# Expert weights in rows of 8 KB, and a nineteenth slot in layer 2's ring of weights

## The chip, the cores and the metric

One core of one Trainium2 chip runs the whole program. The metric is the device time of one execution in microseconds; less is better. The times given are the median of three timed runs, and one further execution was recorded by the hardware profiler.

## What is computed

Two layers of a diffusion backbone over 512 latent tokens of 1024 channels, with 256 context tokens beside them in the first layer. Each layer has four token mixers that are merged by gates, and then a mixture of 16 experts, in which each expert chooses its tokens (64 of the latent tokens, 32 of the context). What the change touches are the weights of the experts:

```
def expert_choice_moe(h, w_router, w_g, w_u, w_d):
    ...
    aff = jax.nn.softmax((h @ w_router).astype(jnp.float32), axis=-1)
    gate, idx = lax.top_k(jnp.swapaxes(aff, 1, 2), cap)
    ...
    xe = h[bidx, idx]
    hid = jax.nn.silu(jnp.einsum('becd,edf->becf', xe, w_g)) * jnp.einsum('becd,edf->becf', xe, w_u)
    ye = jnp.einsum('becf,efd->becd', hid, w_d) * gate[..., None].astype(h.dtype)
    return jnp.zeros_like(h).at[bidx, idx].add(ye)
```

Each of the three matrices of an expert is 1024 by 1024 in float32, 4 MB. One layer's experts are 16 x 3 x 4 MB = 192 MB, all of which has to come from HBM once per layer.

## The kernel before

The experts go in eight pairs, p = 0 to 7. Each pair has a gate, an up and a down product. A weight tile is 1 MB: 256 rows of one expert's matrix, held as 128 partitions of 2 rows of 4 KB. So a product of a pair takes 8 tiles (four quarters of two experts), a pair 24, and a layer 192. `gemm` runs over the quarters; a quarter takes the two experts' tiles, and when it is done it asks for two more tiles (`load_ew(st_ew.i + 2)`, L1117).

`ExpertStream` (L975 on) sets which tile goes where. Its list `loads` has the tiles in the order gate 0, up 0, and then for each pair: gate of the next, down of this one, up of the next. Its list `ring` names the buffers that the tiles use in turn. In layer 1 (`has_c`, the context tokens are there) these are three "raw" buffers and ten of the blocks "b0" to "b9". In layer 2 they are 18: three "raw", "b4", "Xc", then nine blocks, "b10" and three of the tag "ew" in a pool that lives from the output projection to the end of the experts. The tile of number i takes the buffer i modulo 18, and its DMA can go once the matmuls have read the tile that was there.

All of these loads are issued by SyncE (SP), in one order, and those behind one that waits wait too. `ew.load(ew.early)` (L737) asks for the first of them while the output projection is still being computed ("early" is the length of the ring's first part: 5 in layer 2). The coroutine `moe` asks for more when the layer's router runs (L1015), four more that are tied to the router's last result by a one-element copy (L1016), and the rest of the ring tied to the first one-hot matrix of the selection (L1255).

In layer 2 TensorE works on a pair as: up product of p, with the adding of the previous pair's result between its matmuls; gate product of p + 1; down product of p. The down product's result is scaled on VectorE (L1144), split into two parts on ScalarE and VectorE (L201, L202) and added to the tokens by matmuls with one-hot matrices (L1159, L1160). The tokens of a pair come by an indirect DMA from GpSimd (L1070, "xg"). The last down product (p = 7) takes its tiles by halves of columns (`last_gemm`, L1132): such a tile holds 256 rows of 512 columns of both experts, and is loaded by two DMAs of 512 KB.

The inputs may be laid out on the host: `_layout` makes the arrays that lie in HBM. Before, the three expert arrays are passed as they are, [2, 16, 1024, 1024]. The weights of the mixers ("w_in_t", "w_gate_t") are stored there tile by tile already, with 8 KB for each partition.

GpSimd's own DMAs (indirect gathers, stores of the normalized tokens at L800, copies of key parts at L367 and L368) have their descriptors in a scratch area at the start of each partition of SBUF, 16,384 bytes of each by default.

Of the kernel before, what the change touches and what calls it, by code (L numbers as in the profile page):

```python
# [19 lines left out]
L = 2  # L20
D = 1024
KC = 8
NE = 16
# [17 lines left out]
def backbone(ctx: ExitStack, tc: tile.TileContext, A: dict, out: bass.AP):  # L41
    nc = tc.nc
# [4 lines left out]
    def nm(p):  # L47
        cnt[0] += 1
        return f"{p}_{cnt[0]}"

    def pool(name, space=None):
        kw = {"space": space} if space is not None else {"reuse_waits": "tile"}
        return tc.tile_pool(name=nm(name), bufs=1, **kw)

    P0 = ctx.enter_context(pool("p0"))
# [3 lines left out]
    def T_(p, shape, dt=F32, tag=None, bufs=1):  # L59
        t = tag or "t"  # L60
        return p.tile(shape, dt, name=nm(t), tag=tag or nm("u"), bufs=bufs)
# [65 lines left out]
    class Parts:  # L127
        def __init__(self, tiles, per):
            self.tiles, self.per = tiles, per
# [845 lines left out]
    class ExpertStream:  # L975
        def __init__(self, l, has_c):
            self.l, self.pool, self.i, self.t, self.has_c, self.stack = l, None, 0, {}, has_c, ExitStack()
            self.ring = [("raw", 3)] * 3 + ([] if has_c else [("b4", 1), ("Xc", 1)])
            self.early = len(self.ring)
            self.ring += [(f"b{i}", 1) for i in (0, 1, 2, 3, 5, 6, 7, 8, 9)]  # L980
            self.ring += [("b4", 1)] if has_c else [("b10", 1)] + [("ew", 3)] * 3
            self.size = len(self.ring)
            order = [(0, 0), (0, 1)]
            for p in range(8):
                order += ([(p + 1, 0)] if p < 7 else []) + [(p, 2)] + ([(p + 1, 1)] if p < 7 else [])
            self.loads = [(p, mt, qt, e) for p, mt in order for qt in range(4) for e in range(2)]
# [6 lines left out]
        def load(self, upto, after=None):  # L993
            while self.i < min(upto, len(self.loads)):
                key = p, mt, qt, e = self.loads[self.i]
                tag, bufs = self.ring[self.i % self.size]
                t = T_(self.pool if tag == "ew" else P0, [128, 2, 1024], tag=tag, bufs=bufs)
                if after is not None:
                    V.tensor_copy(t[:, 0, 0:1], after)
                src = A[("w_exp_gate", "w_exp_up", "w_exp_down")[mt]]  # L1000
                if (p, mt) == (7, 2):
                    t = t.rearrange("p k (b m) -> p k b m", b=2)
                    rows, cols = (2 * qt + e) % 4 * 256, (2 * qt + e) // 4 * 512
                    parts = [(t[:, ex], src[self.l, 2 * p + ex, rows:rows + 256, cols:cols + 512]) for ex in range(2)]
                else:
                    parts = [(t, src[self.l, 2 * p + e, qt * 256:(qt + 1) * 256, :])]
                for dst, rw in parts:
                    nc.sync.dma_start(dst, rw.rearrange("(k p) m -> p k m", p=128))
                self.t[key] = t
                self.i += 1  # L1010

# [303 lines left out]
    for l in range(L):  # L1315
        n2d = [DR.tile([st.n, D], F32, name=nm("n2"), tag=nm("n2")) for st in (LAT, CTX)]
        ew = ExpertStream(l, l < L - 1)
# [11 lines left out]
def _layout(inp):  # L1329
    f = {k: np.asarray(v) for k, v in inp.items()}  # L1330
    c_ = np.ascontiguousarray
    a = {}
    a["x"] = c_(f["x"][0])
    a["ctx"] = c_(f["ctx"][0])
    cond = np.stack([f["c"][0], f["c_ctx"]])
    a["w_ada"] = c_(f["w_ada"])
    a["b_ada"] = c_(f["b_ada"])

    def pairs(w):
        n = w.shape[2] // 256  # L1340
        return c_(w.reshape(L, KC, 128, n, 2, 128).transpose(0, 3, 2, 4, 1, 5).reshape(L, n, 128, 2048))

    a["w_in_t"] = pairs(f["w_in"])
    a["w_gate_t"] = pairs(f["w_gate"])
    a["w_proj"] = c_(np.concatenate([f["w_pa"], f["w_pb"], f["w_pc"], f["w_pd"]], axis=1))
    a["w_o"] = c_(f["w_o"])
    a["w_sp_t"] = c_(f["w_sp"].transpose(0, 3, 1, 2))
    a["b_sp"] = c_(f["b_sp"])
    a["sgu_ln_g"] = c_(f["sgu_ln_g"])
    a["sgu_ln_b"] = c_(f["sgu_ln_b"])  # L1350
    a["lam_v"] = c_(np.stack([f["lam_q1"], f["lam_k1"], f["lam_q2"], f["lam_k2"]], axis=1))
    for k in ("ln1_g", "ln1_b", "ln2_g", "ln2_b", "w_exp_gate", "w_exp_up", "w_exp_down"):
        a[k] = c_(f[k])
    a["w_router_c"] = c_(f["w_router"].reshape(L, KC, 128, NE).transpose(0, 2, 1, 3))
    cs = np.zeros((128, C_N), np.float32)
    cs[:, C_ID:C_ID + 128] = np.eye(128)
    cs[:, C_TRI:C_TRI + 128] = np.triu(np.ones((128, 128)), 1)
    cs[:, C_IOTA:C_IOTA + 64] = np.arange(64)
    cs[:, C_TOK] = np.arange(128)
    cs[:, C_COND:C_BG] = cond.reshape(2, KC, 128).transpose(2, 1, 0).reshape(128, 16)  # L1360
    cs[:, C_BG:C_CONV] = f["b_gate"].reshape(L * 32, 128).T
    cs[:, C_CONV:C_SUB] = f["conv_w"].reshape(L, 3, 2, 128).transpose(3, 0, 2, 1).reshape(128, 6 * L)
    cs[:, C_SUB:C_LB] = f["subln_g"].T
    cs[:, C_LB:C_N] = f["ln1_b"].reshape(L * KC, 128).T
    for b in range(2):
        cs[:, C_HALF + b] = (np.arange(128) // 32) % 2 == b
    a["consts"] = cs
    t = np.arange(512)
    inv = (np.float32(10000.0) ** (-np.arange(0, 32, 2, dtype=np.float32) / np.float32(32))).astype(np.float32)
    row, col = (t // 64).astype(np.float32), (t % 64).astype(np.float32)  # L1370
    ang = np.concatenate([row[:, None] * inv, col[:, None] * inv], axis=-1).astype(np.float32)
    cos, sin = np.cos(ang).astype(np.float32), np.sin(ang).astype(np.float32)
    p = np.arange(128)
    fr = (p % 64) // 2
    sgn = np.where(p % 2 == 0, -1.0, 1.0).astype(np.float32)
    a["rope"] = c_(np.stack([cos[:, fr].T, sin[:, fr].T * sgn[:, None]], axis=1))
    k = np.arange(64)
    th = 2 * np.pi * ((k[:, None] * k[None, :]) % 64) / 64
    bd = np.zeros((128, 2, 128))
    for g in range(2):  # L1380
        s = slice(64 * g, 64 * g + 64)
        bd[s, 0, s] = np.cos(th)
        bd[s, 1, s] = -np.sin(th)
    a["dft_d"] = c_(bd.reshape(128, 256).astype(np.float32))
    for nme, n in (("l", 512), ("c", 256)):
        k = np.arange(n)
        th = 2 * np.pi * ((k[:, None] * k[None, :]) % n) / n
        cm = np.stack([np.cos(th), np.sin(th)]) / math.sqrt(n * 64)
        a["dft_" + nme] = c_(cm.reshape(2, n // 128, 128, n).transpose(0, 2, 1, 3).reshape(2, 128, -1).astype(np.float32))
    return a  # L1390
# [16 lines left out]
```

## Time and profile before

| | |
|---|---|
| median of three runs | 2636.95 us (2631.57, 2636.95, 2638.67) |
| profiled execution, its own time | 2632.32 us |
| profiled execution, span | 2630.5 us |
| TensorE busy | 2461.1 us, 94% |
| VectorE, ScalarE busy | 1084.4 us, 725.7 us |
| granted TensorE clock, mean | 0.978 |
| DMA | 628.20 MB in 155,842 packets, mean 239 GB/s |

A busy TensorE counts matmuls in flight, so it need not be at its peak. The shares are averages over stages with different limits: layer 1's expert stage lies at about 890 to 1515 us, layer 2's mixers behind it, and layer 2's expert stage from about 2135 us to the end.

### The profile page before, as it was taken

The numbers are of one execution on the slowest core, as the hardware profiler recorded it, in microseconds if no ns is written. First come the engines' busy times: TensorE is split into PE (matmuls) and PEld (weight loads), VectorE is DVE, ScalarE is ACT, GpSimd is POOL, SyncE is SP. The second block draws the span as 40 slices with busy tenths as digits, with TensorE's granted clock in tenths as the row PEclk, the third lists the DMA queues.
The fourth block names the chain that finished last, engine by engine and source line by source line (L and its number), as shares of the span: only waits on it lengthen the run. The fifth ranks groups of instructions, "written<-read, shape, count | busy, mean of one in ns | idle before, by whom it ended". The sixth has DMA issues, their size and how long they took to land. (4 is left out here: it accounts for less than half of the span.)

```text
span 2630.5 us, 35463 instructions
## 1 busy us (share of the span) xinstructions
PE 2461.1 (94%) x14575; PEld 1479.2 (56%) x14575; DVE 1084.4 (41%) x2310; ACT 725.7 (28%) x1400; POOL 210.4 (8%) x247
## 2 busy tenths in 40 slices
PE   6899999999999999999999889999999969988886
PEld 4788876788787333333333277678878733332322
DVE  4656787343237412222221468734322732111114
ACT  3644656332233201010000265633223310000001
POOL 0102121001011000000000002100101100000000
PEclk8899999999999899999999999999999979999998
DMA  7586535222325798888898443552232589999996
GB/s 280 188 296 250 196 111 174 77 96 83 110 80 201 299 408 323 320 307 339 339 349 320 170 136 106 179 202 97 83 110 80 199 349 409 409 409 409 409 409 242
DMA packets 155842, 628.20 MB, mean 239 GB/s; under 512 B 11680, under 2 KB 14112, under 8 KB 137760
## 3 DMA queue, kind: packets, MB, share of 16 engines
q1 hardware_dynamic: 141872, 588.78, 59.3%
q0 software_dynamic: 7520, 23.07, 2.9%
q10 hardware_dynamic: 6288, 14.09, 1.6%
q8 instruction: 114, 1.87, 0.3%
q14 instruction: 48, 0.39, 0.0%
HBM read 608.07 MB, written 10.49 MB: 235 GB/s over the span
## 5 line engine op out<-in xcount | busy, mean ns | idle before, releaser
L1106 PE MATMUL sc<-b,xTl 128*32 128x512 f32 (+1 forms) x2136 | 453.6, 597 | 1.2 <-ACT xTl L286 1.2
L209 DVE TENSOR_TENSOR b<-raw,b 128x512 fp32r<-128x512 f32 x368 | 238.8, 695 | 170.4 <-ACT b L207 168.7
L207 ACT CAST b<-raw 128x512 fp32r<-128x512 f32 x368 | 205.0, 618 | 214.8 <-PE sc L316 124.4
L1106 PEld LDWEIGHTS sc<-b,xTl 128*32 128x32 f32 (+1 forms) x2136 | 119.4, 117 | 201.7 <-issue 196.4
L317 PE MATMUL sc<-b,b 128*128 128x512 f32 x512 | 202.8, 396 | 0.0
L315 PE MATMUL sc<-b,b 128*128 128x512 f32 x512 | 202.3, 395 | 0.0
L316 PE MATMUL sc<-b,b 128*128 128x512 f32 x512 | 202.0, 395 | 0.0
L1106 PE MATMUL sc<-b,hT 128*32 128x512 f32 (+1 forms) x992 | 187.5, 594 | 12.6 <-DMA b<-in_w_exp_down_dram 12.6
L1112 PE MATMUL mm<-b,xTc 128*32 128x512 f32 x776 | 175.2, 593 | 0.3 <-ACT row L273 0.3
L1106 PE MATMUL sc<-raw,xTl 128*32 128x512 f32 (+1 forms) x680 | 157.1, 597 | 0.1
L1144 DVE SCALAR_TENSOR_TENSOR sc<-sc,gsl,row 128x1024 f32<-128x1024 f32 x14 | 18.1, 1293 | 270.7 <-PE sc L1106 270.7
L315 PE MATMUL mm<-b,b 128*128 128x512 f32 (+1 forms) x320 | 124.2, 390 | 3.3 <-DVE lnm L175 2.0
L316 PE MATMUL mm<-b,b 128*128 128x512 f32 (+1 forms) x320 | 123.4, 387 | 0.0
L317 PE MATMUL mm<-b,b 128*128 128x512 f32 (+1 forms) x320 | 123.2, 386 | 0.0
L591 ACT ACTIVATE g<-sc,cst 128x512 f32<-128x512 f32 (+1 forms) x96 | 59.1, 615 | 221.8 <-PE sc L589 221.8
L286 ACT ACTIVATE xTl<-tr,adaC 128x128 f32<-128x128 f32 x64 | 27.5, 455 | 331.4 <-PE tr L1080 167.3
L1167 DVE TENSOR_TENSOR Xl<-Xl,tr 128x512 f32<-128x512 f32 x96 | 62.2, 684 | 134.3 <-PE tr L1160 134.3
L1106 PEld LDWEIGHTS sc<-b,hT 128*32 128x32 f32 (+1 forms) x992 | 52.7, 118 | 104.2 <-issue 79.6
L317 PEld LDWEIGHTS sc<-b,b 128*128 128x128 f32 x512 | 96.4, 188 | 23.0 <-issue 0.5
L153 POOL TENSOR_TENSOR rs_b<-rs_a,mhalf 128x1 f32<-128x1 f32 (+2 forms) x85 | 54.2, 638 | 688.0 <-DVE rs_a L151 400.6
L315 PEld LDWEIGHTS sc<-b,b 128*128 128x128 f32 x512 | 96.3, 188 | 22.8 <-issue 0.5
L316 PEld LDWEIGHTS sc<-b,b 128*128 128x128 f32 x512 | 96.4, 188 | 22.6
(422 smaller groups left out, 4764.0 us busy)
## 6 DMA issues: line engine op xcount, KB each, us to landing
b<-in_w_exp_up_dram SPq DMA_DIRECT2D x87, 1024.0 KB, 12.6
b<-in_w_exp_gate_dram SPq DMA_DIRECT2D x83, 1024.0 KB, 10.3
b<-in_w_exp_down_dram SPq DMA_DIRECT2D x81, 1024.0 KB, 12.6
raw<-in_w_gate_t_dram SPq DMA_DIRECT2D x48, 1024.0 KB, 4.9
raw<-in_w_ada_dram SPq DMA_DIRECT2D x43, 1024.0 KB, 5.6
raw<-in_w_in_t_dram SPq DMA_DIRECT2D x40, 1024.0 KB, 5.2
raw<-in_w_exp_gate_dram SPq DMA_DIRECT2D x27, 1024.0 KB, 8.1
raw<-in_w_exp_up_dram SPq DMA_DIRECT2D x27, 1024.0 KB, 8.7
```

Source lines behind the costliest of these rows:

```text
L153: G.tensor_tensor(r[:, :w], t[:, :w], mhalf[:, :w], ALU.pow)
L207: S.copy(hi[:, c], src[:, c])
L209: V.tensor_sub(lo[:, c], src[:, c], hi[:, c])
L286: S.activation(dst, src, AF.Identity, scale=ada_col(l, ci, st, kc), bias=ada_col(l, si, st, kc))
L315: PE.matmul(ps, hi[:, c, k], h(0, k)[:, :n], start=start and k == k0, stop=False)
L316: PE.matmul(ps, hi[:, c, k], h(1, k)[:, :n], start=False, stop=False)
L317: PE.matmul(ps, lo[:, c, k], h(0, k)[:, :n], start=False, stop=stop and k == k0 + nk - 1)
L591: S.activation(g[:, :n], ps[:, 0, :n], AF.Sigmoid, bias=bgate[l][:, br * 8 + jc:br * 8 + jc + 1])
L1106: PE.matmul(pl[q:q + lw, b, :], lhs_l(k, e)[:, q % 64:q % 64 + lw], weight(p, mt, k, e, b), start=f, stop=s_, tile_position=(0, q))
L1112: PE.matmul(pc[q:q + 32, :], lhs_c(k, e), weight(p, mt, k, e, b), start=f, stop=s_, tile_position=(0, q))
L1144: V.scalar_tensor_tensor(y, y, lat.gs[p], lat.grow, op0=ALU.mult, op1=ALU.mult)
L1167: V.tensor_add(xs, xs, ps)
```

## The change

Three things are changed.

1. The expert arrays lie in HBM tile by tile, [2, 16, 4, 128, 2048]: each tile of 1 MB is one block, and in it each partition has 8 KB in one piece. The last pair's down weights lie there in the halves that `last_gemm` takes, so each of its tiles is one DMA of 1 MB instead of two of 512 KB. What each buffer holds after a load is what it held before.
2. Layer 2's ring has 19 buffers: behind "Xc" comes "ewx", of 8 KB per partition, in the pool of "ew". "early" is 6.
3. The scratch for descriptors of GpSimd's DMAs is 4,096 bytes of each partition instead of 16,384. All SBUF addresses move down by that much.

```
-            self.ring = [("raw", 3)] * 3 + ([] if has_c else [("b4", 1), ("Xc", 1)])
+            self.ring = [("raw", 3)] * 3 + ([] if has_c else [("b4", 1), ("Xc", 1), ("ewx", 1)])
...
-                t = T_(self.pool if tag == "ew" else P0, [128, 2, 1024], tag=tag, bufs=bufs)
+                t = T_(self.pool if tag[:2] == "ew" else P0, [128, 2, 1024], tag=tag, bufs=bufs)
...
-                src = A[("w_exp_gate", "w_exp_up", "w_exp_down")[mt]]
+                dst = t
                 if (p, mt) == (7, 2):
-                    t = t.rearrange("p k (b m) -> p k b m", b=2)
-                    rows, cols = (2 * qt + e) % 4 * 256, (2 * qt + e) // 4 * 512
-                    parts = [(t[:, ex], src[self.l, 2 * p + ex, rows:rows + 256, cols:cols + 512]) for ex in range(2)]
-                else:
-                    parts = [(t, src[self.l, 2 * p + e, qt * 256:(qt + 1) * 256, :])]
-                for dst, rw in parts:
-                    nc.sync.dma_start(dst, rw.rearrange("(k p) m -> p k m", p=128))
+                    dst = t.rearrange("p k (b m) -> p k b m", b=2)
+                nc.sync.dma_start(t.rearrange("p k m -> p (k m)"),
+                                  A[("w_exp_gate", "w_exp_up", "w_exp_down")[mt]][self.l, 2 * p + e, qt])
+                t = dst
...
+    def quarters(w):
+        return c_(w.reshape(L, NE, 4, 2, 128, D).transpose(0, 1, 2, 4, 3, 5).reshape(L, NE, 4, 128, 2 * D))
+
+    for k in ("w_exp_gate", "w_exp_up"):
+        a[k] = quarters(f[k])
+    down = quarters(f["w_exp_down"])
+    tail = f["w_exp_down"][:, NE - 2:].reshape(L, 2, 4, 2, 128, 2, 512)
+    tail = tail.transpose(0, 5, 2, 4, 1, 3, 6).reshape(L, 4, 2, 128, 2 * D)
+    down[:, NE - 2:] = tail.transpose(0, 2, 1, 3, 4)
+    a["w_exp_down"] = down
...
-    nc = bacc.Bacc("TRN2", target_bir_lowering=False, num_devices=1)
+    nc = bacc.Bacc("TRN2", target_bir_lowering=False, num_devices=1, dynamic_dma_scratch_size=4096)
```

The instructions of VectorE, ScalarE and GpSimd stand in the same order as before; on TensorE only the buffers that the matmuls of layer 2's experts read are others. The order moves on SyncE. At the first place, the end of layer 2's output projection, its queue was the last load of the projection's weights, the first expert tiles, and then those that wait for the projection's buffers ("Xc" and "b4" have been asked for further up; a name's first part is the buffer's tag):

```order
L725 DMA raw_15830<-in_w_o_dram 128x2x1024
L1008 DMA raw_15840<-in_w_exp_gate_dram 128x2x1024
L1008 DMA raw_15842<-in_w_exp_gate_dram 128x2x1024
L1008 DMA raw_15844<-in_w_exp_gate_dram 128x2x1024
L1008 DMA b_2597_16195<-in_w_exp_gate_dram 128x2x1024
L1008 DMA b_2598_16197<-in_w_exp_gate_dram 128x2x1024
```

The same place on SyncE now:

```order
L725 DMA raw_15822<-in_w_o_dram 128x2x1024
L1003 DMA raw_15832<-in_w_exp_gate_dram 128x2048
L1003 DMA raw_15834<-in_w_exp_gate_dram 128x2048
L1003 DMA ewx_15842<-in_w_exp_gate_dram 128x2048
L1003 DMA raw_15836<-in_w_exp_gate_dram 128x2048
L1003 DMA b_2598_16189<-in_w_exp_gate_dram 128x2048
```

The extra buffer's tile stands among the first ones, ahead of the third "raw" tile.

The second place is where the ring comes round for the first time in layer 2; on SyncE it was, from the last two tiles of the first round on:

```order
L1008 DMA ew_16505<-in_w_exp_gate_dram 128x2x1024
L1008 DMA ew_16508<-in_w_exp_gate_dram 128x2x1024
L1008 DMA raw_16560<-in_w_exp_gate_dram 128x2x1024
L1008 DMA raw_16562<-in_w_exp_gate_dram 128x2x1024
L1008 DMA raw_16572<-in_w_exp_gate_dram 128x2x1024
L1008 DMA b_2689_16574<-in_w_exp_gate_dram 128x2x1024
L1008 DMA Xc_16584<-in_w_exp_gate_dram 128x2x1024
L1008 DMA b_2691_16586<-in_w_exp_gate_dram 128x2x1024
```

And now:

```order
L1003 DMA ew_16499<-in_w_exp_gate_dram 128x2048
L1003 DMA ew_16502<-in_w_exp_gate_dram 128x2048
L1003 DMA raw_16554<-in_w_exp_gate_dram 128x2048
L1003 DMA raw_16556<-in_w_exp_gate_dram 128x2048
L1003 DMA raw_16566<-in_w_exp_gate_dram 128x2048
L1003 DMA b_2690_16568<-in_w_exp_gate_dram 128x2048
L1003 DMA Xc_16578<-in_w_exp_gate_dram 128x2048
L1003 DMA ewx_16580<-in_w_exp_down_dram 128x2048
```

Before, the eight rows are the eight tiles of pair 1's gate product, two of them in the first round. Now one of these tiles stands a row further up, so three are in the first round, and the eighth row is a tile of pair 0's down product.

## Rows read from the trace of the kernel before

**Rows 1.** The page, 40 equal slices: what the DMA engines moved.

```profile
GB/s 280 188 296 250 196 111 174 77 96 83 110 80 201 299 408 323 320 307 339 339 349 320 170 136 106 179 202 97 83 110 80 199 349 409 409 409 409 409 409 242
```

**Rows 2.** Table by stretch: length, PE, PEld, DVE, ACT, POOL busy, clock, DMA share, GB/s.

```profile
1000.00:1500.00 500.00, 498.46 (x3940) 161.24 (x3940) 126.25 (x246) 48.66 (x85) 7.43 (x8) 1.00 0.82 311
2062.00:2085.00 23.00, 23.00 (x115) 18.68 (x114) 12.54 (x40) 9.73 (x14) 3.42 (x6) 1.00 0.19 69
2125.00:2130.00 5.00, 1.66 (x27) 1.27 (x28) 3.56 (x16) 0.00 (x0) 1.02 (x1) 0.50 0.00 1
2150.00:2287.00 137.00, 131.08 (x588) 45.96 (x586) 30.33 (x55) 12.98 (x21) 2.81 (x3) 1.00 1.03 409
2287.00:2558.00 271.00, 237.16 (x1002) 81.89 (x998) 49.23 (x82) 17.97 (x29) 2.81 (x3) 0.99 1.03 409
```

**Rows 3.** The chain of waits: start us, length us, what; five weight links.

```profile
2128.77 4.72 DMA xg<-n,ixl
...
2287.24 18.78 DMA b<-in_w_exp_down_dram
...
2539.70 18.63 DMA b<-in_w_exp_down_dram
```

**Rows 4.** Timeline of TensorE, pair 6's down product; in brackets the idle time before.

```profile
2548.12 3.69 PE L1106 MATMUL sc<-b,hT 128*64 128x512 f32 x16 [0.60 <-DMA b<-in_w_exp_down_dram]
2553.24 3.65 PE L1106 MATMUL sc<-b,hT 128*64 128x512 f32 x16 [1.43 <-DMA b<-in_w_exp_down_dram]
2558.37 3.22 PE L1106 MATMUL sc<-b,hT 128*64 128x512 f32 x13 [1.48 <-DMA b<-in_w_exp_down_dram]
```

**Rows 5.** TensorE's waits, 2135 to 2612 us: total us, times, longest.

```profile
PE sc L1106 <- DMA b<-in_w_exp_down_dram: 12.6, 10, 1.5
...
PE sc L1106 <- DMA ew<-in_w_exp_down_dram: 1.8, 2, 1.5
...
PE sc L1106 <- DMA raw<-in_w_exp_down_dram: 1.5, 1, 1.5
```

**Rows 6.** Timeline of SyncE's issues: start us, us until the last one.

```profile
2043.83 10.59 SPq L1008 DMA_DIRECT2D raw<-in_w_exp_gate_dram  x3
...
2129.87 0.88 SPq L1008 DMA_DIRECT2D ew<-in_w_exp_gate_dram  x2
2139.82 3.80 SPq L1008 DMA_DIRECT2D raw<-in_w_exp_gate_dram  x3
```

**Rows 7.** DMA packets by size; issues in 8 KB rows: count, KB, us to landing.

```profile
DMA packets 155842, 628.20 MB, mean 239 GB/s; under 512 B 11680, under 2 KB 14112, under 8 KB 137760
...
raw<-in_w_gate_t_dram SPq DMA_DIRECT2D x48, 1024.0 KB, 4.9
raw<-in_w_ada_dram SPq DMA_DIRECT2D x43, 1024.0 KB, 5.6
raw<-in_w_in_t_dram SPq DMA_DIRECT2D x40, 1024.0 KB, 5.2
```

**Rows 8.** Table by stretch: 8 KB rows twice, then the last product's 2 KB rows.

```profile
14.00:26.00 12.00, 6.40 (x32) 0.76 (x32) 3.84 (x9) 0.00 (x0) 1.10 (x2) 0.92 1.01 421
30.00:35.00 5.00, 2.55 (x17) 1.06 (x10) 3.29 (x20) 2.20 (x7) 0.00 (x0) 0.84 1.00 415
...
2580.00:2590.00 10.00, 8.39 (x42) 3.19 (x40) 2.14 (x3) 0.59 (x1) 0.00 (x0) 1.00 1.05 387
```

**Rows 9.** Table by stretch: just behind pair 3's waits.

```profile
2375.00:2380.00 5.00, 4.95 (x14) 1.58 (x15) 1.23 (x1) 0.00 (x0) 0.00 (x0) 0.66 1.02 409
```

**Rows 10.** GpSimd's DMA queue, and its copies of key parts.

```profile
q0 software_dynamic: 7520, 23.07, 2.9%
...
Xl<-Xl POOLq DMA_DIRECT2D x16, 256.0 KB, 3.6
kcE<-kcE POOLq DMA_DIRECT2D x24, 128.0 KB, 3.9
```

More of the change, by code (lines that the diff above doesn't have):

```diff
@@ L1351, in _layout @@
     a["lam_v"] = c_(np.stack([f["lam_q1"], f["lam_k1"], f["lam_q2"], f["lam_k2"]], axis=1))
-    for k in ("ln1_g", "ln1_b", "ln2_g", "ln2_b", "w_exp_gate", "w_exp_up", "w_exp_down"):
+    for k in ("ln1_g", "ln1_b", "ln2_g", "ln2_b"):
         a[k] = c_(f[k])
+    def quarters(w):
[7 more added lines that the diff above has]
+    a["w_exp_down"] = down
     a["w_router_c"] = c_(f["w_router"].reshape(L, KC, 128, NE).transpose(0, 2, 1, 3))
```

## The prediction

> **What bounds the kernel now.** I read the page's 40 slices first [rows 1]: the bytes per second go up and down with the stages, and in seven slices near the end they stand at a flat 409 GB/s. A flat line says that something is full. That is layer 2's expert stage. A table by stretch [rows 2] tells the two expert stages apart. In layer 1's (1000 to 1500 us) TensorE is busy 498.46 of 500 us while the transfers run at 311 GB/s: faster weights buy nothing there. In layer 2's the transfers run at 409 GB/s without a dip from 2150 to 2558 us, and from 2287 on TensorE is busy 237.16 of 271 us. The chain of waits [rows 3] then says where TensorE is held: five times, once in each of the pairs 2 to 6, the chain runs through a transfer of a down weight (18.6 to 18.8 us from issue to landing), and the last such link ends at 2558.33 us; everything behind it is TensorE's own work and the tail. The timeline of one such place [rows 4] shows the form of the wait: the down matmuls want two tiles per step, a step is 3.7 us of matmuls, and two tiles at 409 GB/s take 5.1 us; it adds up to 0.60 + 1.43 + 1.48 = 3.5 us in pair 6. All these waits together come to 12.6 + 1.8 + 1.5 = 15.9 us [rows 5]. So two ceilings hold for any gain from the weights: how much earlier tile 175 (the last down tile of pair 6, counted from 0) lands, and 15.9 us of waits, with what the waits cost in clock on top.
>
> **One tile more in the ring.** Layer 2 asks for its first 18 tiles while the router and the top-k still run; in 2125 to 2130 us the transfers stand still (1 GB/s) [rows 2], the last two go out at 2129.87, and tile 18 is issued only at 2139.82, when TensorE has given back its first slots [rows 6]. With 19 slots one more tile is on its side of that point, and the order shows where: the extra tile is asked for before the last of the three "raw" tiles, whose issues lie between 2043.83 and 2054.42 us [rows 6], ahead of a lull (0.19 of the DMA engines' time in 2062 to 2085 us) [rows 2], so its own transfer is hidden. If that lull were not there it would give the gain back. What remains after 2140 us is one tile shorter: 1.0486 MB at 409 GB/s is **2.56 us**.
>
> **Longer rows.** A tile's partition now takes one run of 8 KB where it took two runs of 4 KB from rows 512 KB apart; the bytes are the same. The kernel already loads 131 tiles in rows of 8 KB (48 + 40 + 43) [rows 7], and the packets of 8 KB and over, 155,842 less 137,760, are 18,082, of which 131 x 128 would be 16,768: such a row goes as one packet. At a full queue these rows run at 421 GB/s (14 to 26 us), the 4 KB rows at 409, and the last gemm's 2 KB rows at 387 [rows 2, 8]. Per tile that is 1.0486 MB / 421 = 2.491 us against 2.564. Between the landing of tile 20, the third of the issues that begin at 2139.82 [rows 6], and that of tile 175 lie 155 tile times; as a check, the 408 us from 2150 to 2558 at 409 GB/s, less six gathers of 0.52 MB, are 156 tiles. One of them is gone with the ring, so 154 x 0.073 = **11.3 us**. Two other rows give the same 421: on one of 16 engines a packet of 2 KB takes 84.7 ns at 387 GB/s and one of 4 KB 160.2 ns at 409, so 2 KB more cost 75.5 ns and a packet has some 9 ns of its own; 8 KB would take 311 ns, which is 421 GB/s. The bounds: a shorter stretch of 8 KB rows gave 415 GB/s [rows 8], so 154 x 0.037 = 5.7 us; without any packet cost it would be 434 GB/s, 154 x 0.148 = 22.8 us, which TensorE could not follow (below). I take 421, the longer stretch.
>
> The Trainium skill has an account of this (DMA: Bandwidth & Descriptors, "Why small descriptors are slow"): some 3 cycles per packet beside one cycle for every 32 bytes. From it I work out, as an estimate, 131 cycles for 4 KB and 259 for 8 KB, so 1.1% per tile; the sum would be 4.5 + 2.6 = 7.1 us. The three rates of rows 2 and 8 differ by more than that, 5.7% and 2.9%.
>
> **What may take some of it back.** At 2128.77 us the first gather runs on the chain, 4.72 us, beside the two "ew" tiles [rows 3, 6]; a neighbour's packet is now twice as long. A gather of 128 rows is 8 packets on each of 16 engines; if each of them waited for 4 KB more, 0.16 us at 409 GB/s over 16 engines, it would cost 1.3 us, and nothing if the "ew" tiles come after it. The two issues lie 1.1 us apart, so most of the gather is ahead: I take 0.3 us and keep 1.3 as the bound. The extra early tile also stands beside the loads of the ln1 rows and the residual; at most 2.6 us later for them, and TensorE has 23 us of 23 to do in 2062 to 2085 [rows 2]; I take nothing, and 2.6 us if that cover failed.
>
> **Is TensorE in the way?** Tile 175 lands 2.56 + 11.3 = 13.9 us earlier. TensorE can follow by 15.9 us [rows 5], and by somewhat more, because its waits also cost it clock: after the waits of pair 3 the granted clock was 0.66 in 2375 to 2380 us [rows 9], the lower of the two levels (1.2 against 2.4 GHz) for most of it, some 1.7 us. That makes 17.6 us the ceiling. So the transfers stay the bound, barely: pairs 2 to 5 should lose nearly all their waits (15.9 - 3.5 = 12.4 us), and pair 6 keeps about 2 us. Behind tile 175 the 16 last tiles take some 41 us (16 x 2.56), and TensorE was not held by a transfer there in the chain, so the tail of 72 us (2630.5 - 2558.3) moves as a block. The eight double issues of 512 KB with 2 KB rows become eight single ones; they lie behind that point and cost or give nothing.
>
> **The sum.** 2.56 + 11.3 - 0.3 = 13.6 us. Against the profiled execution (2632.32 us, of which 2630.5 are span) this gives 2618.7. That execution lies 4.6 us under the median of the three timed runs, 2636.95; the mean of the four is 2634.9, and 2634.9 - 13.6 = **2621**. Its own range is 2.6 + 5.7 - 1.3 = 7.0 up to the ceiling of 17.6 us, so 2617 to 2628, and some 4 us for which runs are drawn.
>
> **Rivals.** (a) *Longer rows give nothing at a deep queue, only the tile counts.* 409 GB/s would then be what memory gives to this stream, and 421 that of another. For it: 409 stands in every full stretch of expert tiles, whatever TensorE does. Against it: two kinds of rows give two rates, and 2 KB a third. It gives 2634.9 - 2.6 = 2632. The Trainium skill would side with it (DMA: Bandwidth & Descriptors, "Specifications"): 512 bytes are enough for line rate, and so 4 KB and 8 KB would be alike; the 387 GB/s of 2 KB rows is not alike. Chance 0.10.
> (b) *Half of it.* The rate is that of the 415 GB/s stretch: 5.7 + 2.6 - 0.3 = 8.0 us, 2627. The same number comes out if TensorE's waits go but other waits move in behind them in pairs 2 to 6 (the split of the down result by ACT). Chance 0.10.
> (c) *Slower: GpSimd's transfers queue for their smaller scratch.* They issue in pairs in the attention (128 and 256 KB, 24 and 16 issues, 3.9 and 3.6 us to landing [rows 10]). If the smaller scratch held only one, the second of each pair would wait for the first: 12 x 3.9 + 8 x 3.6 = 75.6 us, on the path of the keys; wholly exposed, 2621 + 76 = 2697. It is slower than before from the point where over 13.6 us of that, a fifth, reaches TensorE. Against it: that queue moves 7,520 packets in the whole run, 470 for each of 16 engines [rows 10], in 2630 us. Chance 0.04; nothing in the trace shows how full the scratch is. The Trainium skill gives a descriptor 16 bytes (same page, "Terms"); an estimate by it is 256 of them in 4,096 bytes, and a pair would fit.
>
> **How the numbers follow.** The forecast has 0.76, (a) 0.10, (b) 0.10, (c) 0.04. A measurement of this kernel tells about 0.3%, 7.9 us, from no change. Faster by more: the forecast but for its lower edge (0.73), and (b) in about three of four cases, 0.08: together 0.81. Within: the rest of both and (a), 0.15. Slower: (c), 0.04. The range that should hold the time 8 times in 10 is that of the forecast with (b) and the draw of the runs: 2613 to 2630.
>
> **What would show it.** Right: a flat 420 to 423 GB/s in place of 409 in layer 2's expert stage; packets fall from 155,842 to about 102,600; TensorE's waits for down weights fall from 15.9 us to some 2 to 5, those that are left in pair 6; fewer stretches under full clock between 2300 and 2560 us; layer 1's expert stage unchanged in length; the tail behind tile 175 still 72 us. Wrong: still 409 GB/s (a); the waits gone but the gain under 10 us, with new idle time before the split or the transposes (b); idle time of TensorE before the attention's scores (c); or tile 18's successor issued much later than 2140 us, for the start of the stage moves the end one to one.

## The result and the profile after

The changed kernel takes 2619.79 us (median of 5 runs, 2618.48 to 2623.42); the kernel before, timed beside it, took 2636.95. The ratio, which is that of the means, is 0.9942, with a 95% interval of 0.9927 to 0.9956: 15.3 us faster (the medians lie 17.2 us apart), where 2621 us and 13.6 us had been forecast. The profiled execution took 2621.26 us, of which 2619.5 are span.

The page, 40 equal slices, and its line of packets, which answer [rows 1, 7]:

```profile
GB/s 287 185 297 255 191 109 177 77 97 81 113 81 165 299 419 312 318 321 336 346 337 320 164 189 85 171 221 95 90 103 97 146 332 420 421 420 420 421 420 257
DMA packets 102338, 628.20 MB, mean 240 GB/s; under 512 B 11424, under 2 KB 13856, under 8 KB 35104
```

The flat line near the end stands at 420 to 421 GB/s, and the packets are 102,338 (forecast about 102,600). The table by stretch (length, PE, PEld, DVE, ACT, POOL busy, clock, DMA share, GB/s), which answers [rows 2]:

```profile
1000.00:1500.00 500.00, 498.46 (x3944) 161.13 (x3937) 125.68 (x243) 46.70 (x82) 7.73 (x8) 1.00 0.80 310
2062.00:2085.00 23.00, 21.91 (x107) 17.95 (x108) 14.25 (x35) 7.88 (x12) 2.30 (x4) 1.00 0.37 139
2150.00:2287.00 137.00, 130.48 (x578) 45.57 (x575) 28.82 (x50) 12.98 (x21) 1.88 (x2) 0.99 1.01 421
2287.00:2550.00 263.00, 240.76 (x1038) 83.76 (x1034) 50.60 (x87) 17.97 (x29) 4.09 (x4) 0.99 1.01 420
```

Layer 1's expert stage is as it was, 498.46 us of TensorE in 500. The 139 GB/s of 2062 to 2085 us, 69 before, are not the extra tile: the transfers of this execution run some 5 us late there. A later profile of the same kernel (x11 below) runs at almost the times of before, and has 61 GB/s in that stretch; its extra tile, issued at 2049.11 us and landed 7.7 us later, moved just ahead of the lull, where it has 397 GB/s against 323 before:

```profile
2050.00:2062.00 12.00, 10.50 (x46) 8.22 (x45) 8.48 (x15) 1.06 (x3) 0.00 (x0) 1.00 1.00 397
2062.00:2085.00 23.00, 23.00 (x112) 18.69 (x111) 13.70 (x40) 9.73 (x14) 3.42 (x6) 1.00 0.17 61
```

Four links of the chain of waits (start us, length us, what), which answer [rows 3]:

```profile
2053.78 7.59 DMA wrx<-in_w_router_c_dram
...
2134.48 4.58 DMA xg<-n,ixl
...
2141.14 24.77 PE sc L1103 x112
...
2530.38 19.83 DMA Xc<-in_w_exp_down_dram
```

Tile 175 lands at 2550.21 us. It landed at 2558.33 before, only 8.1 us later, since in this execution the stage began later: its first matmul starts at 2141.1 us, and at 2135.5 before. From that matmul to the landing it is 409.1 us, and 422.8 before: **13.7 us less**. The first gather takes 4.58 us (4.72 before). The first link is new: a load of the router's weights.

TensorE's waits on down weights, 2120 to 2612 us (total us, times, longest), which answer [rows 5], and pair 6's down product in the timeline, which answers [rows 4]:

```profile
PE sc L1103 <- DMA raw<-in_w_exp_down_dram: 2.1, 2, 1.3
PE sc L1103 <- DMA Xc<-in_w_exp_down_dram: 1.3, 1, 1.3
PE sc L1103 <- DMA b<-in_w_exp_down_dram: 1.3, 1, 1.3
PE sc L1103 <- DMA ew<-in_w_exp_down_dram: 0.8, 1, 0.8
```

```profile
2540.29 0.64 PE L1103 MATMUL sc<-raw,hT 128*64 128x512 f32 x1 [0.81 <-DMA raw<-in_w_exp_down_dram]
2545.27 3.22 PE L1103 MATMUL sc<-raw,hT 128*64 128x512 f32 x13 [1.32 <-DMA raw<-in_w_exp_down_dram]
2550.26 0.64 PE L1103 MATMUL sc<-Xc,hT 128*64 128x512 f32 x1 [1.33 <-DMA Xc<-in_w_exp_down_dram]
```

They fell from 15.9 to 5.5 us. Of that 3.5 stand in pair 6, as many as before, where the prediction left about 2; pairs 2 to 5 lost all but 2.0. A step of 3.65 us waits 1.32 us for its two tiles: 4.98 us, or 2.49 us for a tile. Issues of SyncE's queue (start us, us until the last), which answer [rows 6]:

```profile
2053.66 0.33 SPq L1003 DMA_DIRECT2D ewx<-in_w_exp_gate_dram  x1
2058.82 0.33 SPq L1003 DMA_DIRECT2D raw<-in_w_exp_gate_dram  x1
...
2145.33 3.76 SPq L1003 DMA_DIRECT2D raw<-in_w_exp_gate_dram  x3
```

Tile 19 is asked for 4.2 us behind the stage's first matmul, as tile 18 was before (2139.82 less 2135.57).

### The profile page after: what moved, and what is told of

Its sections match the earlier page's. It is cut to its first block, busy times and chain, and to the rows that moved or that the text cites. A ratio compares the mean times of both kernels' runs of the same rounds, so it can differ in the third digit from the quotient of the medians.

```text
span 2619.5 us, 35445 instructions
## 1 busy us (share of the span) xinstructions
PE 2463.1 (94%) x14575; PEld 1486.4 (57%) x14575; DVE 1086.0 (41%) x2310; ACT 725.3 (28%) x1400; POOL 210.7 (8%) x247
## 2 busy tenths in 40 slices
DMA packets 102338, 628.20 MB, mean 240 GB/s; under 512 B 11424, under 2 KB 13856, under 8 KB 35104
## 5 line engine op out<-in xcount | busy, mean ns | idle before, releaser
L1103 PE MATMUL sc<-b,xTl 128*32 128x512 f32 (+1 forms) x2144 | 435.0, 597 | 2.7 <-ACT xTl L286 2.7
L1103 PE MATMUL sc<-b,hT 128*32 128x512 f32 (+1 forms) x952 | 178.6, 593 | 1.3 <-DMA b<-in_w_exp_down_dram 1.3
L315 PEld LDWEIGHTS sc<-b,b 128*128 128x128 f32 x512 | 96.3, 188 | 22.9 <-issue 0.5
L596 POOL TENSOR_TENSOR Xl<-Xl,g 128x512 f32<-128x512 f32 x48 | 63.3, 1319 | 537.8 <-DVE g L595 537.8
```

The lines of the kernel that those rows point to most:

```text
L315: PE.matmul(ps, hi[:, c, k], h(0, k)[:, :n], start=start and k == k0, stop=False)
L596: G.tensor_add(m[:, jc, :n], m[:, jc, :n], g[:, :n])
L1103: PE.matmul(pl[q:q + lw, b, :], lhs_l(k, e)[:, q % 64:q % 64 + lw], weight(p, mt, k, e, b), start=f, stop=s_, tile_position=(0, q))
```

## Experiments

Each was timed beside the kernel before on the same chip. Three points are read in each profile: the first matmul of layer 2's experts, the landing of tile 175, and the end. The stage is from the first to the second, the tail from the second to the end. The first point lies between 2132.7 and 2142.4 us in all profiles, and a part of that differs from one execution of a kernel to the next (the three profiles of the changed kernel have 2141.1, 2142.4 and 2136.5); stage and tail don't contain it.

| kernel | median us | ratio, 95% interval | stage us | tail us |
|---|---|---|---|---|
| before | 2636.95 | 1 | 422.8 | 72.2 |
| after | 2619.79 | 0.9942, 0.9927 to 0.9956 | 409.1 | 69.3 |
| x1, ring of 19 alone | 2630.41 | 0.9986, 0.9977 to 0.9995 | 420.9 | 71.1 |
| x2, rows and single issues alone | 2621.28 | 0.9958, 0.9945 to 0.9971 | 412.8 | 71.5 |
| x3, scratch alone | 2634.62 | 1.0003, 0.9993 to 1.0013 | 424.1 | 73.3 |
| x4, rows of 2 KB | 2658.54 | 1.0101, 1.0086 to 1.0115 | 447.2 | 72.2 |
| x5, after, last pair in two issues | 2619.90 | 0.9934, 0.9921 to 0.9948 | 410.5 | 73.2 |
| x6, after, ring of 20 | 2617.09 | 0.9925, 0.9912 to 0.9939 | 407.3 | 69.3 |
| x8, after again | 2618.88 | 0.9939, 0.9926 to 0.9953 | 410.4 | 70.9 |
| x11, after, third time | 2620.31 | 0.9954, 0.9941 to 0.9968 | 409.2 | 69.3 |
| x10, after, router's load first | 2614.36 | 0.9939, 0.9927 to 0.9952 | 409.0 | 69.3 |
| x12, x10 again | 2614.63 | 0.9932, 0.9918 to 0.9945 | 410.2 | 71.0 |
| x9, x6 with router's load first | 2613.50 | 0.9923, 0.9909 to 0.9937 | 407.8 | 70.7 |

The kernel before had 2634.07 us beside x1 to x4, 2634.95 beside x5 to x8, 2632.28 beside x9 and x10, 2632.08 beside x11 and x12.

### One tile more, alone (x1)

The smaller scratch, which makes room for the tile, is in it too; x3 has the scratch alone.

```
-            self.ring = [("raw", 3)] * 3 + ([] if has_c else [("b4", 1), ("Xc", 1)])
+            self.ring = [("raw", 3)] * 3 + ([] if has_c else [("b4", 1), ("Xc", 1), ("ewx", 1)])
...
-                t = T_(self.pool if tag == "ew" else P0, [128, 2, 1024], tag=tag, bufs=bufs)
+                t = T_(self.pool if tag[:2] == "ew" else P0, [128, 2, 1024], tag=tag, bufs=bufs)
...
-    nc = bacc.Bacc("TRN2", target_bir_lowering=False, num_devices=1)
+    nc = bacc.Bacc("TRN2", target_bir_lowering=False, num_devices=1, dynamic_dma_scratch_size=4096)
```

> The kernel before with the ring's nineteenth tile and the 4,096-byte scratch alone; the rows stay 4 KB, the last pair's down weights stay two issues of 512 KB. Forecast: one tile less behind 2140 us at 409 GB/s, so tile 175 lands 2.56 us after fewer tile times; 2634.9 - 2.6 = 2632 to 2634 us, 409 GB/s in layer 2's expert stage, the tail behind tile 175 still 72 us, TensorE's waits on down weights 15.9 - 2.6 or so. Rival, the extra tile's cover fails: no gain, 2637. Rival (c), the smaller scratch holds up GpSimd's transfers: up to 76 us slower. Were the rows to count for nothing and the tile for all, this kernel would take the whole 17 us: 2620.

The transfers and the last weight link of the chain:

```profile
GB/s 282 186 291 255 196 107 178 77 96 80 112 80 184 306 408 326 318 307 339 349 338 323 167 146 108 176 204 97 80 112 80 194 347 409 409 409 409 409 409 248
...
2540.32 18.63 DMA Xc<-in_w_exp_down_dram
```

Still 409 GB/s. The stage is 420.9 us; with the mean of before and x3, 423.4, as the yardstick (both have its order and rows), that is 2.5 us less, one tile at 2.56. The time fell by 0.14% of 2634, 3.7 us, with 1.3 to 6.1 in the interval.

### Longer rows, alone (x2)

```
-            self.ring = [("raw", 3)] * 3 + ([] if has_c else [("b4", 1), ("Xc", 1), ("ewx", 1)])
+            self.ring = [("raw", 3)] * 3 + ([] if has_c else [("b4", 1), ("Xc", 1)])
...
-    nc = bacc.Bacc("TRN2", target_bir_lowering=False, num_devices=1, dynamic_dma_scratch_size=4096)
+    nc = bacc.Bacc("TRN2", target_bir_lowering=False, num_devices=1)
```

The diff is against the changed kernel.

> The changed kernel with 18 tiles in the ring and the scratch as before: only the 8 KB rows and the single issues of the last pair's down weights are left. Forecast: 421 GB/s in layer 2's expert stage and 155 x 0.073 = 11.3 us; with the 2.9 us by which the tail behind tile 175 turned out shorter in the changed kernel, if they come from the single issues, 14.2 us: 2621 to 2624. Rival (a), rows give nothing: 2635 to 2637 and 409 GB/s. Rival (b), half: 2629 to 2631.

```profile
GB/s 285 187 300 257 188 117 169 77 97 81 113 81 185 312 408 323 316 309 336 352 342 319 159 168 95 176 220 97 81 108 85 156 340 421 420 420 420 420 419 244
...
2525.50 19.95 DMA b<-in_w_exp_down_dram
```

The slices of the page and the last weight link: 420 to 421 GB/s with the old ring, and the stage is 10.7 us shorter (forecast 11.3). The time is 11.1 us less (7.6 to 14.5). The two parts add up: 3.7 + 11.1 = 14.8 us, against 15.3, 16.1 and 12.1 in the three comparisons of the changed kernel.

### Smaller scratch, alone (x3)

```
-    nc = bacc.Bacc("TRN2", target_bir_lowering=False, num_devices=1)
+    nc = bacc.Bacc("TRN2", target_bir_lowering=False, num_devices=1, dynamic_dma_scratch_size=4096)
```

> The kernel before with nothing changed but the scratch for GpSimd's DMA descriptors, 4,096 bytes in place of 16,384; every engine's order is that of before. Forecast: no difference (0 us, within 0.3%), copies of key parts 3.9 us and of Xl 3.6 us from issue to landing as before. Rival (c): its transfers queue for scratch, the second of each pair waits for the first, up to 12 x 3.9 + 8 x 3.6 = 76 us slower, with TensorE idle before the attention's scores.

The DMA issues of GpSimd (count, KB each, median us to landing):

```profile
Xl<-Xl POOLq DMA_DIRECT2D x16, 256.0 KB, 3.6
kcE<-kcE POOLq DMA_DIRECT2D x24, 128.0 KB, 3.9
```

The same as in [rows 10], and the time is the same within 0.13%. Rival (c) is out; in x6 the scratch is 2,048 bytes, and that kernel is no slower either.

### Shorter rows (x4)

```
+                nc.sync.dma_start(t.rearrange("p k (b m) -> p (k b) m", b=2),
+                                  src[self.l, 2 * p + e, qt].rearrange("s p m -> p s m"))
...
+        a[k + "_h"] = c_(f[k].reshape(L, NE, 4, 2, 128, 2, 512).transpose(0, 1, 2, 3, 5, 4, 6)
+                         .reshape(L, NE, 4, 4, 128, 512))
```

> The other way along the same line: the kernel before with all expert tiles of both layers (but the last pair's down weights) in rows of 2 KB in place of 4 KB, the same bytes, order and ring. Forecast, if the rate goes by the length of a row: 387 GB/s, 2.71 us for a tile in place of 2.56, 155 x 0.146 = 22.6 us, none of it covered: 2657 to 2660 us, packets up by about 0.07 to 0.1 million; layer 1's expert stage, which moves 311 GB/s, no longer than before. Rival (a), 512 bytes are enough for the full rate and 4 KB rows were as good as 8 KB: no difference, 409 GB/s.

The slices, the packets, the last weight link of the chain, and the largest wait of TensorE on weights in 2150 to 2560 us:

```profile
GB/s 286 201 294 257 173 114 155 92 95 81 110 93 205 290 387 345 321 311 329 335 353 331 116 147 121 221 150 95 81 94 137 230 341 387 387 387 387 387 387 244
DMA packets 250051, 628.20 MB, mean 236 GB/s; under 512 B 11681, under 2 KB 14113, under 8 KB 231969
...
2570.02 14.42 DMA b<-in_w_exp_down_h_dram
...
PE sc L1109 <- DMA b<-in_w_exp_down_h_dram: 17.8, 11, 1.7
```

The same stream, with the same bytes, ring and order, now runs at 387 GB/s; the stage is 23.7 us longer (forecast 22.6) and the time 26.6 us (22.7 to 30.3). So the rate goes with the rows and is not a limit of this stream. The runs of one partition lie apart by another distance in each of the three layouts; row length and spacing were not separated.

### The last pair in two issues again (x5)

```
+                    for ex in range(2):
+                        rw = A["w_exp_last"][self.l, ex, rows:rows + 256, cols:cols + 512]
+                        nc.sync.dma_start(dst[:, ex], rw.rearrange("(k p) m -> p k m", p=128))
```

> The changed kernel, but the last pair's down weights are loaded as before: two DMAs of 512 KB with rows of 2 KB for each of its eight tiles. Forecast of the prediction (the single issues cost or give nothing): 2620, the same as the changed kernel. Theory from the comparison of the two traces: the single issues are what shortened the tail behind tile 175 from 72.2 to 69.3 us, by another order of TensorE's work in the last product; then the tail is some 72 us again and the time 2.9 us longer, 2623. Rival: the tail got shorter through the rate of the other last tiles, or the two loads of ln2 rows that no longer hold up SyncE; then it stays 69 us.

The chain's last weight link; the span of this profile is 2623.3 us:

```profile
2530.27 19.83 DMA Xc<-in_w_exp_down_dram
```

The tail is 73.2 us. Over all profiles but x7's, the five with two issues have 71.1 to 73.3, mean 72.4, and the eight with one 69.3 to 71.5, mean 70.2. So the single issues are worth about 2 us of tail. The profiles show where from. Pair 7's down product, with the additions of its result to the tokens, is in x5:

```profile
2589.20 1.02 PE L1134 MATMUL mm<-ew,hT 128*64 128x512 f32 x2
2590.90 0.73 PE L1161 MATMUL tr<-yeh,ptwl 128*128 128x512 f32 x2 [0.68 <-ACT yeh L201]
```

In the changed kernel:

```profile
2587.66 1.89 PE L1129 MATMUL mm<-ew,hT 128*64 128x512 f32 x8
2589.48 0.51 PE L1156 MATMUL tr<-yeh,ptwl 128*128 128x512 f32 x1
```

With two issues TensorE turns to the additions after two matmuls of the second half, and waits 0.68 us for the split; with one it does eight first, and has no wait there. So TensorE's order did change at this place, and not only the buffers that its matmuls read, as was said ahead of the prediction. From pair 7's transposes to the last addition it is 25.5 to 26.3 us in the five profiles with two issues (25.5 in x1; the other four have a granted clock of 0.55 to 0.60 in its last 3 us, where x1 has 1.00), and 23.7 in all eight with one. What spreads the tails within each group is mainly the clock: in x3, x5, x2, x8, x9 and x12 the granted clock is 0.83 to 0.86 in the 10 us behind tile 175's landing, 1.00 in the other seven, and there it takes 1.4 to 1.7 us longer to those transposes.

The medians don't show the gain (2619.90 against 2618.88 us side by side); one thing that may stand against it is a wait for the router's weights of 0.5 us in layer 2, where the changed kernel has 1.4 to 2.3. It is thus seen in the profiles, and not settled in the times.

### One tile more still (x6)

```
-            self.ring = [("raw", 3)] * 3 + ([] if has_c else [("b4", 1), ("Xc", 1), ("ewx", 1)])
+            self.ring = [("raw", 3)] * 3 + ([] if has_c else [("b4", 1), ("Xc", 1), ("ewx", 2), ("ewx", 2)])
...
-    nc = bacc.Bacc("TRN2", target_bir_lowering=False, num_devices=1, dynamic_dma_scratch_size=4096)
+    nc = bacc.Bacc("TRN2", target_bir_lowering=False, num_devices=1, dynamic_dma_scratch_size=2048)
```

> The changed kernel with one buffer more, a ring of twenty tiles in layer 2, and a scratch of 2,048 bytes to make room. If the transfers still bound the stage: one more tile of 2.49 us, 2617 to 2618, TensorE's waits on down weights 5.5 - 2.5 = 3 us. If TensorE already bounds it (the 5.5 us of waits would be noise of the order): 2620, no change. If the smaller scratch begins to hold up GpSimd's transfers: slower than 2622.

The waits on down weights, 2150 to 2560 us:

```profile
PE sc L1103 <- DMA b<-in_w_exp_down_dram: 5.6, 5, 1.3
```

The stage is 2.3 us shorter than the mean of the three profiles of the changed kernel (409.6), and the medians differ by 1.8 us side by side, within the intervals. The waits on weights did not fall with it: five of up to 1.3 us, 5.6 us in all, where the changed kernel has 5.5. So their sum is not a measure of what an earlier transfer gives.

### Half the weights (x7)

```
+                half = slice(0, 2 if self.has_c else 1)
+                    nc.sync.dma_start(dst[:, half], rw.rearrange("(k p) m -> p k m", p=128)[:, half])
```

> The kernel before, but layer 2's experts load only one half of each weight tile and the matmuls read that half twice: half of layer 2's expert weights are left out, the matmuls are as many as before. It measures TensorE's own pace in layer 2's expert stage. Forecast (TensorE's ceiling 15.9 us of waits and 1.7 us of clock, and a tail that moves as a block): 2634.9 - 17.6 = 2617, no waits on down weights; up to 3 us less if the tail gets shorter as in the changed kernel. If the ceiling is higher (waits also hide work that TensorE could do earlier): under 2612. If the transfers were no bound at all: 2634.

This kernel, which leaves out half of layer 2's expert weights, took 2579.61 us, ratio 0.9788 (0.9774 to 0.9802): 55 us less than before, where the prediction's ceiling was 17.6. First the waits of TensorE in 2150 to 2560 us in this kernel, whole, then the largest of the kernel before that are not on weights:

```profile
PE sc L1108 <- ACT xTl L286: 4.2, 7, 0.6
PE tr L1161 <- ACT yeh L201: 1.5, 1, 1.5
PE tr L1212 <- DVE sg L1203: 1.3, 1, 1.3
PE tr L1161 <- DVE Xl L1167: 0.6, 1, 0.6
PE sc L1134 <- ACT hT L1216: 0.3, 1, 0.3
```

```profile
PE tr L1159 <- ACT yeh L201: 11.4, 5, 2.4
PE tr L1210 <- DVE xTl L284: 5.4, 6, 0.9
```

And the stretch 2287 to 2550 us:

```profile
2287.00:2550.00 263.00, 258.94 (x1139) 90.87 (x1136) 62.66 (x103) 20.16 (x32) 3.75 (x4) 1.00 0.64 223
```

TensorE is busy 258.94 of 263 us; in the changed kernel it is 240.76. But the 55 us are not all the weights'. The edit also gave TensorE another order: in the kernel before, a pair's additions begin two matmuls behind its down product, and TensorE waits for ScalarE's split of that product (yeh); here they begin 16 matmuls behind it, and the split is done by then. Those waits go with the order and not with the weights. The same lines of x4, whose waits on weights are 26.2 us in these 410 us, and of the changed kernel, which has 5.5, show some 2.2 us for each pair in both:

```profile
PE tr L1162 <- ACT yeh L201: 11.4, 5, 2.3
PE tr L1156 <- ACT yeh L201: 13.2, 6, 2.5
```

From the stage's first matmul to pair 7's transposes this kernel takes 401.5 us, and the kernel before 452.0. Of the 50.5 us between them 15.9 are waits on weights, 22.9 are other waits (27.1 before, 4.2 here), and the rest, some 12, is TensorE's busy time (407.8 and 396.0 us). So 55 us is what TensorE has in hand with weights to spare and another order; how much of it the order of before allows was not measured.

### The router's weights ahead (x10, x9, x12, beside x8 and x11)

```
+        wrx = T_(W, [128, 3, KC, NE], tag="wrx")
+        wr = wrx[:, 0]
+        nc.sync.dma_start(wr, A["w_router_c"][l])
         res = T > 2
...
-        wrx = T_(W, [128, 3, KC, NE], tag="wrx")
-        wr = wrx[:, 0]
-        nc.scalar.dma_start(wr, A["w_router_c"][l])
```

The new link in the chain of the changed kernel asks for this test, and the changed kernel was run again to see what differs from one execution to the next.

> The changed kernel once more, as the yardstick for the other three of this call and for where its stage begins. Forecast: 2620, ratio 0.994; layer 2's expert stage begins at 2135 to 2137 us like that of the kernel before, if the 2141 us of its first profile was a draw of that run, and at 2141 us again if the change itself delays it.

> The changed kernel with one load moved: the router's weights (wrx, 64 KB, in both layers) are asked for on SyncE's queue right behind the first expert tile and not on ScalarE's queue behind the split of the last projection weight and beside the expert tiles. Theory: the longer tiles and the extra one together hold that load up, and TensorE's wait for it (the line that reduces the router's weights) grew from 1.9 us in the kernel before to 4.7 and 3.6 us in two profiles of the changed one. Then the waits fall to under 1 us and the time by 2.5 to 4 us, 2615 to 2616. Rival: the wait is given back before the expert stage by what TensorE waits for next (the loads of the ln1 rows and the residual): under 1 us, 2619.

> The same move on top of the ring of twenty tiles, for which 2617.1 us and 4.1 us of such waits were measured. Theory: 2613 to 2614. Rival (given back by the next wait): 2617.

> The changed kernel beside the one with the router's load moved, on the same chip, since the kernel before drew 2632.3 us in one call and 2635.0 in the other and so the two ratios (0.9939 both) can't be told apart from 2614.4 against 2618.9 us. Forecast: 0.994 of before; waits for the router's weights 3.5 to 4.7 us in the two layers.

> The changed kernel with the router's load on SyncE's queue behind the first expert tile, once more, beside the changed kernel. Theory (the wait reaches the end): 2.5 to 4 us less than that kernel on the same chip, waits 0.7 us. Rival (it is given back): less than 1 us.

TensorE's wait for the router's weights in layer 2, 2040 to 2080 us: of before, of the changed kernel, of x10:

```profile
PE tr L810 <- DVE wrk L808: 0.4, 1, 0.4
```

```profile
PE tr L810 <- DVE wrk L808: 1.4, 1, 1.4
```

```profile
PE tr L810 <- DVE wrk L808: 0.5, 1, 0.5
```

The load takes 64 KB. From its issue to its landing it takes 4.2, 3.4 and 3.8 us in before, x3 and x2 (4.7 in x4), 5.7 in x1, and 7.6, 8.5, 7.7, 8.1 and 6.7 in the kernels that have both the extra tile and the long rows (after, x8, x11, x6, x5). It is issued 0.1 us behind the extra tile. TensorE waits for it 0.4 to 0.5 us in the kernels without the one or the other and 1.4, 2.3, 1.5, 1.7 and 0.5 in those five. Moved ahead of the second expert tile, it costs 0.5 again, and in layer 1 0.2 us, where the wait had been 1.5 before and 3.3, 1.3 and 1.4 in the three profiles of the changed kernel. The stage's first matmul stands at 2132.7, 2133.9 and 2135.8 us in the three kernels with the load moved, at 2136.5 to 2142.4 in the five with tile and rows but not the move, and at 2132.7 to 2138.4 in the others.

x10's first comparison could not be read against x8's, which was made on another chip: the ratios were alike (0.9939), the medians 4.5 us apart. Side by side on one chip (x12 and x11) it is 2614.63 against 2620.31 us, 5.7 us, somewhat more than the waits; the two intervals overlap by 0.0004. The ten runs of x10 and x12, all on that chip, have a median of 2614.5; the sixteen of the changed kernel, on several, 2619.6. Against the kernel before beside them the ratios are 0.9939 and 0.9932 with the move, and 0.9942, 0.9939 and 0.9954 without: 2.5 us on the mean. That the move pays is thus likely, its size open. x9, which has it on top of the ring of twenty, has the lowest median, 2613.50 us (0.9923), some 6 us under the changed kernel's; its interval overlaps two of that kernel's three.

## Why the prediction was right, point by point

**What bounds the kernel: right.** Four kernels changed the rate or the number of the transfers in layer 2 and nothing else in that stage, and the stage followed each: one tile -2.5 us (forecast 2.56), 8 KB rows -10.7 (11.3), 2 KB rows +23.7 (22.6), both parts -13.8 (409.6 on the mean of three profiles; 13.9).

**The rate of long rows: right.** 421 GB/s was read from another load of the kernel [rows 8]. Rivals (a) and (b) had 409 and 415; x2 shows 420 to 421, and x4 has 387 with the expert tiles themselves. Nor did other waits move in, the second form of (b): from the stage's first matmul to tile 175, TensorE's waits on anything but weights are 24.3 us before and 23.5 in the changed kernel. The 0.3 us for the gather did not show, as told below. By the Trainium skill's account (DMA: Bandwidth & Descriptors, "Why small descriptors are slow") the prediction had estimated 1.1% per tile; 421 against 409 is 2.9%, and the measurement decides. The Trainium skill's 512 bytes for line rate (same page, "Specifications") don't hold for this stream: 387, 409 and 421 GB/s at 2, 4 and 8 KB.

**The tail "moves as a block" and the single issues "cost or give nothing": too coarse.** The tail became about 2 us shorter (72.4 to 70.2 us). With single issues the scheduler puts the last product's additions in another order among its second half's matmuls, and the last matmuls end earlier behind tile 175. x5 brings the old order and the old tail back.

**The cover of the extra early tile: mis-sized.** The prediction took nothing and kept 2.6 us; it named the ln1 rows and the residual as those that might suffer, and looked for packets that wait behind longer ones at the gather. The gather did not suffer (4.3 to 4.6 us in all these profiles, 4.72 before). The load that did is the router's: it took some 4 us longer and TensorE waited 1 to 2 us more, in layer 2 always but for x5. The extra tile moved just ahead of the lull and not in it, and pushed back what was issued there.

**The ceiling of 17.6 us: too low, as far as the runs show, and without effect on the sum.** TensorE's waits on weights fell from 15.9 us to 5.5, 5.9 and 6.8 in the three profiles of the changed kernel, and the stage by 13.8. A part of the rest is TensorE's busy time in the stage, 383.4 us on the mean of before and x3 and 380.1 on that of the changed kernel, where the prediction had put 1.7 us of clock for all its waits. x6 has a stage 16.1 us shorter than the yardstick and still 5.6 us of waits on weights. So the transfers were still the bound, and not "barely"; how much TensorE could follow in this order stays open, since x7's 55 us come with another order. The low end of the forecast's own range, 2617 us, rested on that ceiling.

**The sum.** 13.8 us in the stage and 2.2 in the tail, less some 1.3 for the router's weights in layer 2 (the mean wait of 1.7 us less 0.4) and 0.5 in layer 1 (2.0 less 1.5), make 14.2 us; the three comparisons gave 15.3, 16.1 and 12.1. The waits vary between profiles, so the small terms are rough. The forecast of 13.6 left out the gain of the tail and the loss at the router, which nearly cancel: that it came so close is in part luck.

## What to carry to other kernels

Where the transfers of a stage stand at a flat rate, look in the same trace for loads with other row lengths at a full queue: their rates gave the gain of a new layout to within 1 us in 11, and laying each tile out as one run per partition costs nothing on the chip. A buffer more in a ring is worth one tile's transfer, but ask which small load is issued beside the tile that now goes earlier, and put that load ahead of it. The sum of the waits that a profile puts down to a late transfer does not measure what an earlier one gives: in x1 they fell by 4.2 us and the stage by 2.5, in the changed kernel by about 10 and 13.8, and in x6 the stage fell by another 2.3 and they stayed as they were. A run with the transfers made short shows how far the other engine could go only if its order of work is still the same, as it was not in x7.

## What the runs showed of the hardware

- The rate of a full queue of 1 MB loads into 128 partitions goes with their rows: 387 GB/s at 2 KB, 409 at 4 KB, 420 to 421 at 8 KB (their length and their spacing were not separated).
- A 64 KB load issued 0.1 us behind a 1 MB load takes 7.6 to 8.5 us to land where the rows of the big loads are 8 KB (6.7 in one profile), 5.7 where they are 4 KB, and 3.4 to 4.7 where the last big load was issued 2.5 us ahead of it.
- GpSimd's DMAs took the same 3.6 and 3.9 us with a quarter of the scratch for descriptors.
